# v projected with tokens on partitions, and the second projection's seven products in another order

## The chip, the cores and the metric

The kernel runs on one core of a Trainium2 chip. The metric is the device time of one execution in microseconds (us). Times are medians of several executions on the chip; the profile is one execution more, recorded by the hardware profiler, with a time of its own.

## The reference

One layer of a decoder trunk, all in float32, with 1024 tokens (S) of width 1024 (D). Two branches share one input projection:

```python
mod = silu(c) @ ada_w + ada_b;  shift, scale, gate = split(mod, 3)
h = rms_norm(x, norm_w) * (1 + scale) + shift
gm_u, gm_v, gm_z, ssm_z, xbc, dt_raw, g_a, g_b = split(h @ w_in)
# gMLP branch: layer norm of v over its 1024 columns, then a causal mix over chunks of 128 tokens, per group of 128 columns
v   = layer_norm(gelu(gm_v), gm_ln_w, gm_ln_b)
y_a = gelu(gm_u) * (einsum('gts,bnsgd->bntgd', tril(gm_ws), v) + gm_bs) * silu(gm_z)
# SSD branch: conv, silu, chunked state passing (8 groups, 32 heads), gate, rms norm per group of 256 columns
xbc = silu(causal_depthwise_conv(xbc, conv_w, conv_b))
y_b = (ssd_scan(x, softplus(dt_raw + dt_bias), ...) + x * d_skip) * silu(ssm_z)
y_b = rms_norm(y_b per group, ssm_norm_w)          # width 2048
merged = sigmoid(g_a) * (y_a @ w_proj_a) + sigmoid(g_b) * (y_b @ w_proj_b)
out = rms_norm(x + gate * (merged @ w_out), final_norm_w)
```

The layer norm of v needs, for each token, the mean and variance over all 1024 columns of gelu(v); the mix contracts over the tokens of a chunk, so it wants v with tokens on the 128 partitions.

## The kernel before, in words

**Products.** Large matrix products are split in two ways. Each float32 operand is a sum of a rounded part h and a rest l, and a product is h·h + l·h + h·l, three matmuls on 128x512 tiles. Above that stands a Strassen scheme with seven products instead of eight of half the size (p1 to p7), with sums of the quarters as operands: on the activations' side b11, b22, b21 and t1 to t4, on the weights' side a11, a12, a22 and s1 to s4. One product over 512 rows of the contraction is 12 matmuls (3 times 4 blocks k of 128).

**Stages.** In order of time TensorE does: the norm, the modulation and the first gate products; the input projection; the state passing (SSD) with the first projection (y_a @ w_proj_a) between its steps; the second projection (y_b @ w_proj_b); the output projection, followed by the last norm and the stores.

**Input projection.** A job is a pair of 128-column blocks of w_in (`pair`), made by seven `product` calls, each 12 matmuls at line 574. The weights are the stationary operand, the activations (transposed, tokens along the free dimension) the moving one, so the result has columns on partitions: c1 and c2, 128x1024 each. `pair_weights` loads four 256 KB tiles for a pair (rows of 128 columns, 512 B pieces) and forms the operands on ScalarE (rounded part) and VectorE (rest, line 523, and the sums). The four v pairs come first (v0, v2, v4, v6), then those for B and C, u and z, x, z and the gates.

**v.** `v_done` (L849) applies gelu and hands the block to `v_natural` (L857) twice, some products later (`later(n, f)` calls f after n products; `run_tasks` counts). `v_natural` turns four 128x128 blocks on TensorE into a PSUM bank (tile pv, L84), takes statistics of each on VectorE (L863), copies the bank on ScalarE (L864) and, for the second half, stores v_d[g], 512 KB. `v_stats` (L868) aggregates over the 8 groups; `mix_load` and `mix` read v_d, normalise and mix.

**SSD and its row sums.** For each group `post2` sums squares on TensorE (16 tiny matmuls into a bank called pq), scales on VectorE (L1117) and takes the power -1/2 on POOL (L1121); `post3` turns the 128x8 result into a row on TensorE (pr, L84) and stores it as rs_d[g]. The last two groups (6 and 7) do this within p1 of the second projection.

**Second projection.** 56 units (nm, k), L1418: seven products in the order p1, p5, p2, p3, p6, p7, p4, eight blocks k each. A unit is 12 matmuls (L1477): four PSUM banks, three matmuls a bank. `loads` runs 6 units ahead, `operands` 4. A product uses four banks x or four banks y; p1, p6, p7 and p4 take x, p5, p2 and p3 take y. Fresh quarters of y_b are loaded (yb_d), normalised with the row factors (L1416) and kept in slots; sums of quarters (S and T forms) are made on VectorE. After the last k of a product the banks are copied out (ScalarE) or added to a kept tile (VectorE, L1630 for p2, L1643 for p7). `merged` applies the gates and forms the operands of the output projection. `tha` (L1308) is the end of the first projection's gating: VectorE reads PSUM banks called pma there.

**What sets the order.** TensorE's matmuls and turns stay in the written order. On VectorE, ScalarE and POOL a scheduler orders the instructions by a timeline of its own, except those pinned (`pin`) or given high priority; each engine then executes its list in order. Loads are issued by SP (L90) in its list's order, stores mostly by ScalarE (L93). A load waits until the slot of its pool that it is to fill has been released.

## Time and profile before

| | |
|---|---|
| runs, us | 1407.88, 1404.68, 1408.73 (median 1407.88) |
| profiled execution, us | 1407.67 |
| its span, us | 1405.9 |
| granted clock of TensorE | 0.997 |
| DMA over the span | 283.37 MB, mean 202 GB/s |

The span runs from the first to the last instruction of the profile; the execution's own time is 1.8 us longer. Rows of the timeline give start and duration in us, the engine (PE is TensorE, PEld its weight loads, DVE VectorE, ACT ScalarE, SP the engine that issues loads), the line, the operation, output and inputs by name, the tile, and how many instructions are joined; in brackets the idle time just before and what ended it. A run of matmuls overlaps, so the distance of two starts is the cost of one, not its duration.

### The profile page before, as it was taken

What the parts mean: (1) busy time and instruction counts of PE and PEld (TensorE: products, weight loads), DVE (VectorE), ACT (ScalarE), POOL (GpSimd) and SP (SyncE); (2) the same over time, 40 slices, a digit from 0 to 9 for tenths busy, and PEclk for the clock granted to TensorE, in tenths of its full rate; (3) what the DMA queues carried; (4) which work ended last, traced back from release to release, by engine and by line L of the source; (5) the groups of instructions that cost most, each with busy time, mean ns of one, the idle gap of its engine ahead of it and who ended that gap; (6) DMA issues with size and microseconds to landing.
All of it is one profiled execution on the core that took longest, in us unless ns stands there. A gap on an engine that the chain in (4) does not pass through costs nothing.

```text
span 1405.9 us, 20633 instructions
## 1 busy us (share of the span) xinstructions
PE 1377.1 (98%) x7035; PEld 1139.9 (81%) x7035; DVE 1062.4 (76%) x1863; ACT 797.0 (57%) x1471; POOL 213.0 (15%) x208
## 2 busy tenths in 40 slices
PE   8999999999999999999999999999999999999997
PEld 6688888888888888888887888888888877878886
DVE  4786776777778889889788796388667767876976
ACT  5764576556656665556565555677766723322443
POOL 0000000000000011111000010038778740000001
PEclk9999999999999999999999999999999999999999
DMA  8653343343344777787675774598778749878903
GB/s 263 173 165 98 113 120 105 105 121 120 116 125 134 214 202 239 236 248 232 192 221 156 240 214 135 173 353 318 262 253 296 275 168 328 320 231 296 350 33 120
DMA packets 273150, 283.37 MB, mean 202 GB/s; under 512 B 15341, under 2 KB 223637, under 8 KB 273045
## 3 DMA queue, kind: packets, MB, share of 16 engines
q1 hardware_dynamic: 185684, 198.52, 44.4%
q10 hardware_dynamic: 87360, 83.54, 17.8%
q8 instruction: 55, 0.90, 0.3%
q14 instruction: 51, 0.41, 0.1%
HBM read 194.55 MB, written 87.46 MB: 201 GB/s over the span
## 4 chain that ended last, share of the span: by engine, by line
PE 80%; DMA 8%; DVE 5%; POOL 2%; issue 2%; ACT 1%; SPq 1%; ACTq 0%; DVEq 0%; POOLq 0%
PE xcb L574 6%; PE xuz L574 6%; PE xz L574 6%; PE xx L574 5%; PE xg L574 5%; PE x L1477 4%; PE yp L1477 4%; PE ox L1676 3%; PE yuz L574 3%; PE ycb L574 3%; PE pma L81 3%; PE xv L574 3%; PE yz L574 3%; PE yg L574 3%; PE yx L574 3%; DMA dcy<-acs_d 3%
## 5 line engine op out<-in xcount | busy, mean ns | idle before, releaser
L793 POOL TENSOR_TENSOR wog<-wog,gb 128x256 f32<-128x256 f32 x16 | 18.3, 1159 | 676.6 <-PE zz L574 413.3
L1007 ACT ACTIVATE dcy<-dcy,nacs 128x128 f32<-128x128 f32 x256 | 78.6, 388 | 14.9 <-POOL dcy L1002 14.5
L1002 POOL TENSOR_SCALAR_AFFINE_SELECT dcy<-dcy 128x1024 f32<-128x1024 f32 x32 | 35.0, 1095 | 135.7 <-ACT ea L999 132.3
L999 ACT ACTIVATE ea<-dcy 64x512 f32<-64x512 f32 x64 | 40.1, 626 | 14.2 <-DMA dcy<-acs_d 13.8
L920 ACT ACTIVATE ac<-ac 128x1024 f32<-128x1024 f32 x32 | 33.9, 1060 | 23.0 <-DVE ac L918 22.8
L81 PE MATMUL pma<-yh,wah 128*128 128x512 f32 x128 | 43.3, 419 | 0.0
L1027 DVE TENSOR_TENSOR dcy<-dcy,pc 128x1024 f32<-128x1024 f32 x32 | 39.0, 1218 | 4.8 <-PE pc L84 3.0
L81 PE MATMUL pma<-yh,wal 128*128 128x512 f32 x128 | 42.5, 413 | 0.0
L1089 POOL TENSOR_TENSOR yz<-y,sl 128x512 f32<-128x512 f32 x32 | 41.4, 1295 | 1.1
L1087 DVE TENSOR_TENSOR ym<-yn,ea 128x512 f32<-128x512 f32 (+1 forms) x32 | 19.9, 622 | 28.5 <-PE yn L81 28.3
L81 PE MATMUL pma<-yl,wah 128*128 128x512 f32 x128 | 40.1, 394 | 0.0
L1088 POOL TENSOR_TENSOR y<-y,ym 128x512 f32<-128x512 f32 (+1 forms) x32 | 36.6, 1144 | 14.4 <-DVE ym L1087 14.4
L81 PEld LDWEIGHTS yn<-sl,st 128*128 128x128 f32 x224 | 30.3, 190 | 8.3 <-issue 4.4
L81 PE MATMUL yn<-sl,st 128*128 128x128 f32 x224 | 31.6, 276 | 4.9 <-DVE st L1057 4.9
L1416 DVE SCALAR_TENSOR_TENSOR yn<-yn,par,rb 128x512 f32<-128x512 f32 x32 | 24.0, 749 | 15.7 <-DMA yn<-yb_d 15.5
L81 PE MATMUL sp<-xe,bn 128*128 128x256 f32 x112 | 32.6, 408 | 3.3 <-DVE ssq L1117 1.7
L81 PE MATMUL yi<-dcy,xd 128*64 128x128 f32 x512 | 35.7, 283 | 0.0
L918 DVE SCALAR_TENSOR_TENSOR ac<-c2x,cwt,ac 128x1023 f32<-128x1023 f32 (+2 forms) x24 | 31.2, 1300 | 5.3 <-ACT ac L916 5.1
L918 DVE SCALAR_TENSOR_TENSOR ac<-c2cb,cwt,ac 128x1023 f32<-128x1023 f32 (+2 forms) x24 | 31.1, 1296 | 4.4 <-ACT ac L916 4.3
L1691 POOL TENSOR_TENSOR r<-r,fnw 128x512 f32<-128x512 f32 x2 | 2.5, 1296 | 203.7 <-DMA out_dram<-r 203.7
L1055 POOL TENSOR_TENSOR st<-st,cd 128x256 f32<-128x256 f32 x48 | 32.1, 668 | 8.0 <-PE yn L81 5.3
L918 DVE SCALAR_TENSOR_TENSOR ac<-c1cb,cwt,ac 128x1023 f32<-128x1023 f32 (+2 forms) x24 | 31.6, 1318 | 1.3 <-ACT ac L916 1.3
(2980 smaller groups left out, 4390.9 us busy)
## 6 DMA issues: line engine op xcount, KB each, us to landing
sl<-s_d SPq DMA_DIRECT2D x32, 768.0 KB
s_d<-ac ACTq DMA_DIRECT2D x32, 512.0 KB
dcy<-acs_d SPq DMA_DIRECT2D x32, 512.0 KB
aw<-in_ada_w_dram SPq DMA_DIRECT2D x16, 512.0 KB
wbr<-in_w_proj_b_dram SPq DMA_DIRECT2D x64, 128.0 KB
wb_d<-wbb ACTq DMA_DIRECT2D x32, 256.0 KB
wb_d<-wbc ACTq DMA_DIRECT2D x32, 256.0 KB
yb_d<-yz ACTq DMA_DIRECT2D x32, 256.0 KB
```

What stands on the lines that cost most here:

```text
L81: pin(PE.matmul(acc, l, r, start=first, stop=last))
L574: pin(PE.matmul(ps, lw[:, k * P : (k + 1) * P], r[k], start=first and n + k == 0, stop=n == 2 and k == 3, skip_group_check=not first))
L918: V.scalar_tensor_tensor(ac[:, s:], cc[:, : S - s], conv_wt[:, 3 - s, i : i + 1], ac[:, s:], op0=ALU.mult, op1=ALU.add)
L920: A.activation(ac, ac, AF.Silu)
L999: A.activation(ea[hh * HD : (hh + 1) * HD], dcy.rearrange("p (j e) i l -> p e j (i l)", e=2)[hh * HD : (hh + 1) * HD, hh], AF.Exp)
L1002: G.affine_select(out=d8, in_=d8, compare_op=ALU.is_ge, fill=-1e30, base=0, pattern=[[0, 2 * HPG], [1, P]], channel_multiplier=-1)
L1007: A.activation(dcy[:, h, i, :], dcy[:, h, i, :], AF.Exp, bias=sub[:, i, h : h + 1])
L1027: V.tensor_tensor(d3, d3, pc[:, 0:256].unsqueeze(1).to_broadcast([P, HPG, 256]), op=ALU.mult)
L1088: G.tensor_add(y1[:, :, t0:], y1[:, :, t0:], m[:, :, t0:])
L1089: G.tensor_mul(yz, y1, sl[:, 4:6])
L1477: pin(PE.matmul(ps[j], a[:, v, js], r, start=first and n + k == 0, stop=n == 2 and k == KT - 1, skip_group_check=not first))
L1676: pin(PE.matmul(ps, a[:, tsl], b[:, cs], start=first and n + j == 0, stop=n == 2 and j == 3, skip_group_check=not first))
```

## The change

1. **v.** The four v pairs are replaced by `v_block`. Blocks of the activations are now the stationary operand and rows of w_in (128x512 tiles, 256 KB, 2 KB pieces) the moving one, so the result has tokens on partitions. The same seven products run over 28 units (product, k) in the order p1, p5, p6, p3, p7, p2, p4, each unit 12 matmuls on four banks. Sums of the weights' quarters are made in place in the 8 slots (four of them are kept from p5 to p3); quarters are loaded again where they are needed again, 36 loads of 256 KB instead of 16. The turns of `v_natural`, its copies and its stores go; gelu works on the finished wide tiles, 16 statistics of 512 columns replace 64 of 128, and 16 stores of 256 KB (512 B pieces) fill v_d. `pair_weights` and the loop over the pairs lose their special case for the first pairs.
2. **Row sums.** The scaling in `post2` gets high priority. Groups 6 and 7 do `post2` after units 1 and 2 of p1 (before: 1 and 4) and `post3` after units 3 and 4 (before: 4 and 6).
3. **Second projection.** The order becomes p1, p3, p6, p5, p7, p2, p4, on the banks x, y, x, y, x, y, x. The sums of quarters are formed in place (b12-b11, b22-b12, then b22-b11 and b21-b22), the sums of results too: p1, p3 and p5 are copied out, p6, p5, p7 and p2 added to kept tiles. Banks are taken as three of y, four of x, and the last of y, so pma's banks fall to other positions. `merged` goes through a21, a22, a11, a12, with s1, s2, s3 formed accordingly.

The core of the diff (new and changed lines of `v_block`, `post2`, and the second projection):

```diff
-    def v_done(g):
-        def done(cv):
-            A.activation(cv, cv, AF.Gelu_apprx_tanh)
-            vn = wide(f"vn{g}")
-            later(3 if g < 6 else 2, v_natural, g, cv, vn, 0)
-            later(4 if g < 6 else 3, v_natural, g, cv, vn, 1)
-        return done
-    def v_natural(g, cv, vn, q):
-        pt = bank(f"pv{g}_{q}")
-        for i in range(4):
-            ch = 4 * q + i
-            tp(pt[:, i * P : (i + 1) * P], cv[:, ch * P : (ch + 1) * P], ident)
-        for i in range(4):
-            V.bn_stats(bst[:, 4 * q + i, g, :], pt[:, i * P : (i + 1) * P])
-        A.copy(vn[:, q * 512 : (q + 1) * 512], pt)
-        if q:
-            store(v_d[g], vn)
+    def v_block():
+        V_OPS = (("p1", "b11", "x"), ("p5", "t1", "y"), ("p6", "t2", "x"), ("p3", "b22", "y"), ("p7", "t3", "x"),
+                 ("p2", "b21", "y"), ("p4", "t4", "x"))
+        units = [(nm, k) for nm, _, _ in V_OPS for k in range(4)]
...
+            if nm == "p5":
+                keep(V.tensor_add(t, q[0], t))
+                kept[k] = t
+            elif nm == "p6":
+                t = kept[k]
+                keep(V.tensor_sub(t, t, q[0]))
+            elif nm == "p3":
+                t = kept.pop(k)
+                keep(V.tensor_sub(t, q[0], t))
+            elif nm == "p7":
+                keep(V.tensor_sub(t, q[0], t))
+            hi, lo = wt(f"{nm}v{k}h", "wh", 8), wt(f"{nm}v{k}l", "wl", 8)
+            keep(A.copy(hi, t))
+            keep(V.tensor_sub(lo, t, f32(hi)))
...
+        def ahead():
+            while loaded[0] < len(units) and live[0] + (2 if units[loaded[0]][0] in ("p5", "p7") else 1) <= 8:
+                loads(loaded[0])
+                loaded[0] += 1
+        LEAD = 3
...
+        def finished(nm, i):
+            rows, c = (0, 4)[nm[2] == "2"] + 2 * i, (0, 1)[nm[1] == "2"]
+            w = res[nm][i]
+            A.activation(w, w, AF.Gelu_apprx_tanh)
+            for j in range(2):
+                V.bn_stats(bst[:, rows + j, c, :], w[:, j * 512 : (j + 1) * 512])
+                store(v_d[4 * c : 4 * c + 4].rearrange("g p q -> p g q")[:, :, (rows + j) * P : (rows + j + 1) * P],
+                      w[:, j * 512 : (j + 1) * 512].rearrange("p (g q) -> p g q", g=4))
...
+        for u, (nm, k) in enumerate(units):
+            for j in range(4):
+                js = slice(j * P, (j + 1) * P)
+                (bh, bl), (wh, wl) = (bop[bn][v][k] for v in range(2)), wops[u]
+                for n, (l, r) in enumerate(((bh, wh), (bl, wh), (bh, wl))):
+                    pin(PE.matmul(ps[pn][j], l[:, js], r, start=nm in ("p1", "p5", "p2") and n + k == 0,
+                                  stop=n == 2 and k == 3, skip_group_check=nm not in ("p1", "p5", "p2")))
...
-            V.tensor_scalar(ssq[:, g * NCH + q * 4 : g * NCH + q * 4 + 4], pq[:, 0:4], 1.0 / 256, EPS,
-                            op0=ALU.mult, op1=ALU.add)
+            with tc.high_priority():
+                V.tensor_scalar(ssq[:, g * NCH + q * 4 : g * NCH + q * 4 + 4], pq[:, 0:4], 1.0 / 256, EPS,
+                                op0=ALU.mult, op1=ALU.add)
...
-    units = [(nm, k) for nm in ("p1", "p5", "p2", "p3", "p6", "p7", "p4") for k in range(KT)]
+    units = [(nm, k) for nm in ("p1", "p3", "p6", "p5", "p7", "p2", "p4") for k in range(KT)]
-    fresh = {"p1": (0, 0), "p5": (0, 1), "p2": (KT, 0), "p3": (KT, 1)}
+    fresh = {"p1": (0, 0), "p3": (KT, 1), "p6": (0, 1), "p2": (KT, 0)}
...
-        if nm == "p5":
+        if nm == "p6":
             V.tensor_sub(b12, b12, b11)
-        elif nm == "p6":
-            V.tensor_sub(b12, b22, b12)
-            give(f"yn{KT + k}_1")
+            V.tensor_sub(b22, b22, b12)
         elif nm == "p7":
-            V.tensor_sub(b11, b12, b11)
+            V.tensor_sub(b11, b22, b11)
...
+        elif nm == "p2":
+            give(f"p2r{k}")
+            V.tensor_sub(b21, b21, b22)
+            give(f"yn{KT + k}_1")
...
-    GATES = {"p2": (0, 0), "p6": (0, 1), "p7": (4, 1), "p4": (4, 0)}
+    GATES = {"p5": (0, 1), "p7": (4, 1), "p2": (0, 0), "p4": (4, 0)}
...
-                psy = banks("yp5", "y")
+                psy = banks("yp3", "y", 3)
                 psx = banks("x", "x")
-                rows_bank[0] = lambda name: psy[("pr6", "pr7", "pq6_1", "pq7_1").index(name)]
-            elif nm in ("p2", "p3"):
+                psy += [psb.tile([P, 512], F32, name="yp33", tag="by3")]
+                rows_bank[0] = lambda name: psy[("pq6_1", "pq7_1", "pr6", "pr7").index(name)]
+            elif nm in ("p5", "p2"):
                 psy = banks(f"y{nm}", "y")
...
-        if nm == "p1" and k in (1, 4):
-            late = groups[NG - 2 + k // 4]
+        if nm == "p1" and k in (1, 2):
+            late = groups[NG - 3 + k]
             late.post2(1, late.late)
...
-        if nm == "p1" and k in (4, 6):
-            groups[NG - 4 + k // 2].post3()
+        if nm == "p1" and k in (3, 4):
+            groups[NG - 5 + k].post3()
```

232 lines of the change are left out of this document (130 added, 102 removed).

## The prediction

> **What bounds the kernel now.** I read the page first, for which engine sets the end. In its fence stand the busy time of each engine and the shares of the chain that ended last.
>
> ```profile
> PE 1377.1 (98%) x7035; PEld 1139.9 (81%) x7035; DVE 1062.4 (76%) x1863; ACT 797.0 (57%) x1471; POOL 213.0 (15%) x208
> ...
> PE 80%; DMA 8%; DVE 5%; POOL 2%; issue 2%; ACT 1%; SPq 1%; ACTq 0%; DVEq 0%; POOLq 0%
> ```
>
> TensorE is busy for 1377.1 of the 1405.9 us of the span and carries 80% of the chain. An edit therefore moves the end by the TensorE time that it adds or takes away, or by a wait of TensorE that it makes or removes; work on other engines counts only where TensorE waits for it. The profiled run took 1407.67 us, 0.21 under the median of 1407.88 of the runs shown (1404.68 to 1408.73), so the sum below is made against 1407.67. A change under 0.3% (4.2 us) can't be told from none.
>
> The next view is the timeline of TensorE in the v pairs. A row is start, duration, engine, line, and how many instructions it joins.
>
> ```profile
> 90.05 1.07 PE L574 MATMUL yv<-t1h,p5v2h 128*128 128x512 f32 x4
> ...
> 92.77 0.60 PE L84 MATMUL pv<-ident,c1v 128*128 128x128 f32 x4
> 93.12 1.17 PE L574 MATMUL xv<-t4h,p4v0h 128*128 128x512 f32 x4
> ...
> 95.96 0.60 PE L84 MATMUL pv<-ident,c1v 128*128 128x128 f32 x4
> ```
>
> One product of a pair is twelve matmuls of 128x512 in three rows of four. The product that begins at 90.05 ends where the pv row begins: 2.72 us, 0.227 each. The one that begins with the pv row at 92.77 ends at 95.96, where the next pv begins: 3.19. A group of four turns costs TensorE 0.47 us. All that this stage does besides is seen in the rows of the tile pv (minimum, median and maximum ns, first and last start).
>
> ```profile
> L863 DVE BATCH_NORM_STATS2 bst<-pv x64: 278/282/293, 95.3 to 166.5; 128x6 f32<-128x128 f32 x64
> L84 PE MATMUL pv<-ident,c1v x32: 270/272/275, 92.8 to 161.8; 128*128 128x128 f32 x32
> ...
> L84 PE MATMUL pv<-ident,c2v x32: 270/272/273, 104.6 to 165.4; 128*128 128x128 f32 x32
> L864 ACT COPY vn<-pv x16: 578/587/589, 96.2 to 166.8; 128x512 f32<-128x512 f32 x16
> ```
>
> Last come the windows, for what the other engines and the transfers have left (busy time of PE, PEld, DVE, ACT and POOL, the granted clock, the DMA share, GB/s).
>
> ```profile
> 100.00:170.00 70.00, 70.00 (x337) 57.47 (x337) 46.45 (x124) 35.17 (x56) 0.00 (x0) 1.00 0.34 110
> ...
> 1178.50:1200.00 21.50, 19.81 (x89) 16.07 (x88) 18.93 (x32) 9.01 (x17) 1.65 (x1) 1.00 1.04 393
> ...
> 1222.00:1245.00 23.00, 21.07 (x90) 16.20 (x89) 22.32 (x38) 7.05 (x12) 0.00 (x0) 1.00 0.76 274
> ```
>
> In the v stage VectorE is busy 46 of 70 us and the transfers use a third of their time. In the second projection VectorE is full in one window (22.32 of 23 us), and 393 GB/s has been moved in another. The clock is 1.00 in all.
>
> **The change, part by part.**
>
> *v with tokens on partitions.* The 28 units of the new block hold 12 matmuls each, the same 336 of 128x512 as the four pairs. Whether an operand is the stationary or the moving one doesn't alter their count or shape, and I take 0.227 us each; a unit is 2.72. The 64 turns in 16 groups go: 16 x 0.47 = 7.5 us off TensorE. With them go 16 copies on ScalarE and 48 of 64 statistics on VectorE (the 16 left are four times as wide); both engines were ahead, so these count nothing. Added are 20 loads of 256 KB on SP, so that 9.4 MB are read instead of 4.2, and the eight stores of 512 KB become 16 of half the size on ScalarE's queue. The extra 5.2 MB over 76 us are 68 GB/s on the 110 of the window, 178 in sum, less than half of the 393 seen; the price there is zero unless the slots run dry, which is the first rival.
>
> *The start of the block.* In the kernel before, the first product needs the rounded-off rest of its weights (p1v0l) only at its ninth matmul.
>
> ```profile
> 70.54 1.07 PE L574 MATMUL xv<-b11h,p1v0h 128*128 128x512 f32 x4
> ...
> 76.45 1.07 PE L574 MATMUL xv<-t2h,p6v0h 128*128 128x512 f32 x4
> ```
>
> From 70.54 to 76.45 are two products, 5.91 us where 5.44 would do, so 0.47 was lost already. The new first unit takes its three matmuls bank by bank, so the rest is needed by the third matmul, at 70.54 + 2 x 0.227 = 71.0.
>
> ```profile
> 71.58 0.69 DVE L523 TENSOR_TENSOR p1v0l<-a11v,p1v0h 128x512 fp32r<-128x512 f32 x1
> 72.18 0.68 DVE L529 TENSOR_TENSOR s1v<-a21v,a22v 128x512 f32<-128x512 f32 x1
> ```
>
> VectorE comes to it at 71.58, in the same place of its order in both kernels, and is done at 72.27. With the time to start, TensorE resumes near 72.3: 1.3 us lost instead of 0.47, +0.85. The second unit's rest takes the next place, 72.18, and is done near 72.9; it is needed after 74.5. The operands that follow have over a unit in hand.
>
> *The first product of the second projection.*
>
> ```profile
> 1156.92 0.39 PE L1477 MATMUL x<-p1bh,p1a 128*128 128x512 f32 x1
> ...
> 1158.74 0.39 PE L1477 MATMUL x<-p1bh,p1a 128*128 128x512 f32 x1
> 1160.54 0.50 PE L1477 MATMUL x<-p1bh,p1a 128*128 128x512 f32 x1 [1.41 <-DVE tha L1308]
> ```
>
> ```profile
> 1159.81 1.28 DVE L1308 SCALAR_TENSOR_TENSOR tha<-tha,pma 128x512 f32<-128x512 f32 x2
> ```
>
> The tenth matmul opens the fourth bank and waits 1.41 us, since that bank still holds pma of group 7, which VectorE reads from 1159.81 on. In the new order of banks pma's bank is that of the third instead, three matmuls earlier. The wait ends when it did and begins 3 x 0.227 sooner: +0.68.
>
> *The row sums of groups 6 and 7.* The chain is a VectorE scaling, POOL's power, a turn on TensorE.
>
> ```profile
> 1175.78 0.27 PE L84 MATMUL yp<-ident,ssq 128*8 128x128 f32 x1
> ...
> 1183.21 0.27 PE L84 MATMUL yp<-ident,ssq 128*8 128x128 f32 x1 [1.69 <-POOL ssq L1121]
> ```
>
> ```profile
> 1174.59 0.68 DVE L1456 TENSOR_TENSOR p1bl<-yn,p1bh 128x512 fp32r<-128x512 f32 x1
> ...
> 1181.27 0.15 DVE L1117 TENSOR_SCALAR ssq<-yp 128x4 f32<-128x4 f32 x1
> ```
>
> ```profile
> 1181.51 1.65 POOL L1121 TENSOR_TENSOR ssq<-ssq,nhalf 128x8 f32<-128x8 f32 x1 [12.90 <-DVE ssq L1117]
> ```
>
> TensorE waits 1.69 us at 1183.21 since the scaling stood late in VectorE's order: done 1181.42, then POOL 1.65 us to 1183.16. The change asks for both sums earlier (after units 1 and 2 instead of 1 and 4) and the turns after units 3 and 4. The scaling then stands behind the eighth p1bl, which began at 1174.59 and gives way about 0.6 later (as 71.58 to 72.18 above), so 1175.2 + 0.15; with the same 0.1 and 1.65 the power is ready near 1177.1. TensorE reaches the second turn after five units and both sums, the point at which it stands at 1175.78 in the row above, plus 0.68 from the bank, some 1176.5. A wait of 0.65 is left: -1.05. Ends: -1.69 (no wait) and 0.
>
> *The borders between products.*
>
> ```profile
> 1229.38 0.39 PE L1477 MATMUL yp<-p2bh,p2a 128*128 128x512 f32 x1
> 1230.41 0.47 PE L1477 MATMUL yp<-p3bh,p3a 128*128 128x512 f32 x1 [0.64 <-issue]
> ...
> 1231.56 0.50 PE L1477 MATMUL yp<-p3bh,p3a 128*128 128x512 f32 x1 [0.22 <-DVE c L1630]
> ...
> 1233.36 0.50 PE L1477 MATMUL yp<-p3bh,p3a 128*128 128x512 f32 x1 [0.84 <-DVE c L1630]
> ...
> 1234.56 0.49 PE L1477 MATMUL yp<-p3bh,p3a 128*128 128x512 f32 x1 [0.23 <-DVE c L1630]
> ```
>
> After p2's last matmul at 1229.38 the next could begin at 1229.61; the tenth matmul of p3 begins at 1234.56, where 9 x 0.227 = 2.04 would put it at 1231.65. So 2.9 us are lost: p3 takes the banks of the product just ahead, and VectorE, full in that window, is late in adding p2 up from them. The new order alternates x,y,x,y,x,y,x; each set of banks has a whole product, 21.8 us, to be emptied, and no such wait is left: -2.9.
>
> ```profile
> 1298.06 0.39 PE L1477 MATMUL x<-p4bh,p4a 128*128 128x512 f32 x1
> ...
> 1300.57 0.51 PE L1477 MATMUL x<-p4bh,p4a 128*128 128x512 f32 x1 [0.24 <-DVE p L1643]
> ```
>
> Likewise p4 behind p7: the tenth matmul starts at 1300.57 and could have at 1298.06 + 2.04 = 1300.10, so -0.5. In the new order p2 stands between them.
>
> The sums in place move VectorE's and ScalarE's work about, not its amount by more than a few instructions. In p7, p2 and p4 I count about 110 VectorE instructions of 128x512 in the changed file. The full window above did 38 in 22.32, 0.59 each, so 110 take 64.6 us beside 24 x 2.72 = 65.3 of TensorE: full, but operands lead by four units (10.9 us), so I take nothing, with an upper end in the second rival. Between the stages both kernels have the same order on every engine; the state passing and the output projection I leave as they are.
>
> **Sum:** -7.5 + 0.85 + 0.68 - 1.05 - 2.9 - 0.5 = -10.4, which gives 1407.67 - 10.4 = **1397.3 us**, 0.7% faster. With the free ends (no wait at the start and none at the turn) it is -11.9, 1395.8; with no gain at the turn 1398.3.
>
> **Rivals.**
>
> *The v block runs dry (slower).* Its 28 units share eight slots. In p5 to p3 four of them are held by sums kept in place, and p7 loads two quarters a unit; a load starts only when VectorE has freed a slot, and SP issues in order, so one late release holds back all behind it.
>
> ```profile
> 62.23 0.50 SPq L90 DMA_DIRECT2D a22v<-in_w_in_dram  x1
> 62.78 0.50 SPq L90 DMA_DIRECT2D a12v<-in_w_in_dram  x1
> ...
> 1167.27 0.32 SPq L90 DMA_DIRECT2D yn<-yb_d  x1
> ```
>
> ```profile
> 1169.90 0.75 DVE L1416 SCALAR_TENSOR_TENSOR yn<-yn,par,rb 128x512 f32<-128x512 f32 x1 [3.01 <-DMA yn<-yb_d]
> ```
>
> A 256 KB load issued at 1167.27 let VectorE go on at 1169.90: 2.6 us. A unit that sees a whole landing loses 2.6. The gain is eaten up at 4 such units, and from 6 on the kernel is slower by more than 0.3%; if the eight units of p3 and p7 wait, 8 x 2.6 = 20.8, and 1397.3 + 20.8 = 1418. Against it: SP issues such loads 0.55 us apart (62.23, 62.78), so landings overlap; and each load is asked for when the operand four units earlier has been formed, 10.9 us ahead, four landings long. Chance 0.13. [...]
>
> *VectorE sets the pace in p7, p2, p4 (no change).* At 0.69 us each, the whole duration of the VectorE row at 71.58, the 110 take 75.9, 10.6 over TensorE's 65.3. If the lead is used up when p7 begins, all is given back: 1407.9. For it: the full window in p3. Against: that window kept 0.59, and the products p3, p6, p5 ahead ask less. Chance 0.07.
>
> *The borders don't gain (smaller gain).* The second projection's waits come back elsewhere: both turns wait as long as before, and p6, whose units load 256 KB of y, as much of row factors every other time and 512 KB of weights just behind p3's like loads, starts as late as p3 did. Then only the v part counts, with the bank: -7.5 + 0.85 + 0.68 = -6.0, 1401.7. For it: at 0.92 MB in 2.72 us that is 337 GB/s, above the first and third of the windows shown; against: 393 GB/s were moved without starving TensorE of operands. Chance 0.10.
>
> **How the numbers follow.** My forecast has 0.70: the terms are waits that the trace shows, each with its cause removed, and the largest is work taken off the engine that is full. Faster is that and the third rival, 0.80; same is the second, 0.07; slower is the first, 0.13. The range: at the low end 1395.8 less 3.0 for the lower of the runs shown (1404.68 against 1407.67), 1392.8; at the high end it takes in the third rival with 1.1 of run spread (1408.73 against 1407.67) and the part of the second in which half the lead is lost, 1397.3 + 5.3 = 1402.6, so 1403. That leaves out the first rival and half of the second, under 2 in 10.
>
> **What would show it.** No pv tile, one wait of TensorE near 1.3 for p1v0l and none after it until the block ends, near 70.5 + 28 x 2.72 + 1.3 = 148. In the second projection a wait of about 2.1 at p1's seventh matmul, one under 0.9 at the second turn, none at the borders; the output projection as long as before. A wait of TensorE on v's quarters with a DMA behind it would make the forecast wrong by the first rival; VectorE waits at p2's or p4's units by the second; more time per matmul with swapped operands (over 0.227) by none of them, at 3.4 us for each hundredth.

## The result, and the profile after

The changed kernel takes 1402.55 us (median of 9 runs) against 1407.0 for the kernel before beside it: ratio 0.9967, 95% interval 0.9952 to 0.9983. A second set gave 1402.41, 0.9966 (0.9954 to 0.9978). It is faster, by 4.5 to 5.7 us in the medians where 10.4 were predicted, and not for the reason that the sum gave the most weight to. The profiled execution took 1405.65 us with a span of 1403.9; that of the repeat (e1) took 1401.54, which is nearer to the median.

The v block did in its place what the prediction said. Its start and its end in TensorE's timeline of the changed kernel:

```profile
70.47 0.40 PE L914 MATMUL vx<-p1v0h,b11h 128*128 128x512 f32 x1
...
72.25 0.50 PE L914 MATMUL vx<-p1v0l,b11h 128*128 128x512 f32 x1 [1.15 <-DVE p1v0l L850]
...
147.85 0.39 PE L914 MATMUL vx<-p4v3l,t4h 128*128 128x512 f32 x1
148.08 1.07 PE L536 MATMUL xcb<-b11h,p1cb0h 128*128 128x512 f32 x4
```

One wait, for p1v0l, and none up to the end at 148.08, against the 148 written down.

The second projection runs from its first matmul to the first of the output projection (`ox`); the last row is the only wait of TensorE that the list of waits has between the two.

```profile
1160.21 0.39 PE L1548 MATMUL x<-p1bh,p1a 128*128 128x512 f32 x1
...
1162.92 0.50 PE L1548 MATMUL x<-p1bh,p1a 128*128 128x512 f32 x1 [1.19 <-DVE tha L1378]
...
1176.26 0.27 PE L84 MATMUL yp<-ident,ssq 128*8 128x128 f32 x1
...
1179.20 0.27 PE L84 MATMUL yp<-ident,ssq 128*8 128x128 f32 x1
...
1318.08 0.39 PE L1741 MATMUL ox<-ma11h 128*128 128x512 f32 x1
```

```profile
PE x L1548 <- DVE tha L1378: 1.2, 1, 1.2
```

It lasts 157.87 us instead of 163.51 (1156.92 to 1320.43): -5.64. No wait is left at a border, and none at the turns.

What the prediction did not look at lies between the two. Four pairs by the start of their first product, before and then after:

```profile
194.51 0.84 PE L574 MATMUL xx<-b11h,p1x0h 128*128 128x512 f32 x3
...
513.52 1.07 PE L574 MATMUL xx<-b11h,p1x4h 128*128 128x512 f32 x4
...
684.88 1.07 PE L574 MATMUL xz<-b11h,p1z3h 128*128 128x512 f32 x4
...
898.73 1.07 PE L574 MATMUL xg<-b11h,p1g14h 128*128 128x512 f32 x4
```

```profile
188.49 0.84 PE L536 MATMUL xx<-b11h,p1x0h 128*128 128x512 f32 x3
...
511.31 1.07 PE L536 MATMUL xx<-b11h,p1x4h 128*128 128x512 f32 x4
...
687.18 1.07 PE L536 MATMUL xz<-b11h,p1z3h 128*128 128x512 f32 x4
...
900.36 0.84 PE L536 MATMUL xg<-b11h,p1g14h 128*128 128x512 f32 x3
```

The changed kernel is 6.02 us ahead at x0, 2.21 at x4, and 2.30 behind at z3. From x4 to z3 lie nine pairs; before they take 171.36 us, 19.04 each, with no wait at all; after 175.87. The waits of TensorE between 460 and 720 us, of which the kernel before has none in this profile, say where:

```profile
PE xuz L536 <- DVE c2uz L552: 1.9, 1, 1.9
PE xz L536 <- DVE c2z L552: 1.4, 2, 1.1
PE xcb L536 <- DVE c2cb L552: 1.0, 1, 1.0
PE xx L536 <- DVE c2x L552: 0.5, 1, 0.5
```

All are of one kind. A pair's product p4 is held back until p1 and p5 of the next pair are done, and adds to the bank from which VectorE has first to take p7 (the addition c2<-p5,x). That addition comes too late. The largest, in VectorE's timeline and then in TensorE's:

```profile
465.00 1.29 DVE L726 SCALAR_TENSOR_TENSOR gacc<-ag,sc,gacc 128x1024 f32<-128x1024 f32 x1 [3.60 <-DMA ag<-in_ada_w_dram]
466.21 1.28 DVE L984 SCALAR_TENSOR_TENSOR ac<-c2x,cwt,ac 128x1022 f32<-128x1022 f32 x1
...
474.40 0.68 DVE L552 TENSOR_TENSOR c2uz<-p5uz,xuz 128x512 f32<-128x512 f32 x1
```

```profile
475.13 1.81 PE L536 MATMUL xuz<-t4h,p4uz7h 128*128 128x512 f32 x4 [1.89 <-DVE c2uz L552]
476.74 1.91 PE L536 MATMUL xuz<-t4l,p4uz7h 128*128 128x512 f32 x4
478.45 1.30 PE L536 MATMUL xuz<-t4h,p4uz7l 128*128 128x512 f32 x4
479.59 0.62 PE L536 MATMUL xcb<-t2h,p6cb4h 128*128 128x512 f32 x2
```

VectorE stands 3.60 us for a load of the gate's weights (ag), has work without a gap from 465.00 on, and reaches the addition at 474.40. In the kernel before the list is the same and the wait is 0.65:

```profile
468.10 1.28 DVE L764 SCALAR_TENSOR_TENSOR gacc<-ag,sc,gacc 128x1024 f32<-128x1024 f32 x1 [0.65 <-DMA ag<-in_ada_w_dram]
```

TensorE's wait of 1.89 us lies ahead of x4 and belongs to this execution: in e1 VectorE stands 1.48 us for the same load, TensorE does not wait, and x0 to x4 takes 319.06 us, against 319.01 before and 322.82 in the profile of after. The waits that the list has behind x4 come to 2.9 us of the 4.51 lost there. A wait in the list is idle time only; at cb5, for one of 0.99, p4 starts 1.15 us late and the row behind it another 0.13.

So the profile of after is accounted for: -6.02 to x0, +7.65 from there to g14, +1.66 in the state passing, -5.64 in the second projection, +0.35 behind it: -2.0, the 1405.65 against 1407.67. The repeat e1: -5.99, +4.17, -1.09, -3.06, -0.1.

### The profile page after: what moved, and what is told of

Same layout as the page of the kernel before. It is cut to its first block, busy times and chain, and to the rows that moved or that the text cites. A ratio compares the mean times of both kernels' runs of the same rounds, so it can differ in the third digit from the quotient of the medians.

```text
span 1403.9 us, 20510 instructions
## 1 busy us (share of the span) xinstructions
PE 1371.6 (98%) x6971; PEld 1134.5 (81%) x6971; DVE 1053.8 (75%) x1815; ACT 787.1 (56%) x1459; POOL 212.4 (15%) x208
## 4 chain that ended last, share of the span: by engine, by line
PE 67%; DMA 13%; DVE 9%; ACT 4%; issue 4%; POOL 2%; SPq 2%; ACTq 0%; DVEq 0%; POOLq 0%
PE xuz L536 6%; PE x L1548 6%; PE xcb L536 5%; PE yp L1548 5%; PE xx L536 4%; PE xz L536 4%; DMA wbr<-in_w_proj_b_dram 3%; PE vx L914 3%; PE xg L536 3%; PE yuz L536 3%; PE ycb L536 3%; PE pma L81 2%; PE ox L1741 2%; DMA dcy<-acs_d 2%; PE yx L536 2%
## 5 line engine op out<-in xcount | busy, mean ns | idle before, releaser
L948 ACT ACTIVATE vm<-vm,vr 128x128 f32<-128x128 f32 x64 | 25.8, 484 | 14.0 <-DMA vm<-v_d 13.5
```

## The experiments

"The middle" is the stretch from x4 to z3, whose undisturbed length is 171.36 us; "loss" is what is over that. "Margin" is the time from the end of VectorE's addition of p7 to the start of p4. For the pair z2, before and then after, VectorE's row and TensorE's:

```profile
630.32 0.67 DVE L590 TENSOR_TENSOR c2z<-p5z,xz 128x512 f32<-128x512 f32 x1
```

```profile
633.20 1.07 PE L574 MATMUL xz<-t4h,p4z2h 128*128 128x512 f32 x4
```

```profile
633.52 0.67 DVE L552 TENSOR_TENSOR c2z<-p5z,xz 128x512 f32<-128x512 f32 x1
```

```profile
634.25 1.19 PE L536 MATMUL xz<-t4h,p4z2h 128*128 128x512 f32 x4 [1.11 <-DVE c2z L552]
```

Before, p4 starts 2.21 us after the addition has ended; after, it waits 1.11 and starts 0.06 behind it. All the profiles:

| kernel | time as a ratio to before (95% interval) | loss in the middle | margin from z1 to g6 |
|---|---|---|---|
| before (profile; e4) | 1 | 0.0; 1.3 | 2.0 to 3.9; 0.2 to 2.0 |
| after; e1 | 0.9967; 0.9966 | 4.5; 5.3 | 0.05 to 0.4; 0.05 to 0.3 |
| e2 v alone | 1.0014 (0.9998, 1.0029) | 6.4 | 0.05 to 0.3 |
| e3 second projection alone | 0.9964 (0.9951, 0.9977) | 1.2 | 1.5 to 3.8 |
| e5 after, padded | 1.0003 (0.9990, 1.0017) | 3.2 | 0.05 to 0.4 |
| e6 before, fewer turns | 1.0023 (1.0005, 1.0040) | 3.5 | 0.05 to 1.7 |
| e16 before, padded | 1.0069 (1.0047, 1.0091) | 0.7 | 0.05 to 2.4 |
| e17 after, same count | 1.0030 (1.0012, 1.0049) | 4.9 | 0.04 to 0.4 |
| e9 after, one tap | 0.9932 (0.9916, 0.9947) | 0.0 | 3.0 to 4.6 |
| e10 e3, one tap | 0.9951 (0.9938, 0.9964) | 0.0 | 2.9 to 4.1 |
| e7; e8 GpSimd sums | 0.9963; 0.9977 | 4.6; 6.3 | 0.04 to 0.8; 0.05 to 0.2 |
| e11; e12 fewer transfers | 0.9951; 0.9989 | 3.5; 2.2 | 0.05 to 1.0; 0.05 to 0.8 |
| e13; e14 p4 later | 1.0056; 1.0068 | other waits | 5.2 to 6.1; 5.1 to 6.1 |
| e15 all three | 1.0061 | other waits | 3.2 to 5.2 |
| e18 one piece | 0.9970 (0.9953, 0.9987) | 6.1 | 0.05 to 2.4 |

**The change again, its parts, and the kernel before again.** e2 has v_block alone, e3 the order of the second projection and the priority of the row sums' scaling alone.

```diff
 e2:    units as before   ("p1", "p5", "p2", "p3", "p6", "p7", "p4")     v_block()
 e3:    units as changed  ("p1", "p3", "p6", "p5", "p7", "p2", "p4")     jobs v0, v2, v4, v6 as before
```

> The changed kernel once more, nothing altered, for a second profile. In the first profile its v part (from 70.5 us to the start of pair x0) came out 6.0 us shorter and its second projection 5.6 us shorter than before, but pairs z0 to g8 (about 467 to 690 us) lost 8.3 us and the state passing 1.7 us, on instruction orders that are the same in both kernels. Theory N (landings vary from run to run, the loss is a draw): the v part and the second projection repeat within 0.5 us, the loss in the middle comes out elsewhere and by another amount, and the times spread over more than 5 us. Theory S (the loss belongs to the kernel): the waits for c2uz, c2cb, c2z and c2x return at the same pairs, loss between 6 and 10 us again. Time by either about 1402.5, within 1398 to 1407.

> Only v with tokens on partitions; second projection, its order, banks and the row sums as before. If the parts add and the middle is undisturbed: -6.0, ratio 0.9957. Theory S, the loss in the middle (7.6 us in the profile) comes with the v block: -6.0 + 6 to 8, ratio 1.000 to 1.0015, and the waits at 475 and 594 us show in the profile. Theory N: some loss in some runs, ratio about 0.998.

> Only the second projection's order with its banks and row sums; v by pairs and turns as before. The profile should show p1 to the output projection 5.6 us shorter (157.9 instead of 163.5). Theory S (loss from the v block): -5.6, ratio 0.996, and the pairs from z0 to g8 as in the kernel before. Theory N: ratio 0.996 to 0.998, with waits in the middle in some runs.

> The kernel before once more, nothing altered, for a second profile: how far one program's middle (pairs z0 to z7, then the state passing) moves from one profiled execution to the next. Theory N: starts of the pairs differ by several us between its two profiles, beginning with a landing. Theory S: they agree within 1 us.

Measured: e1 1402.41, e2 1409.22, e3 1401.84, against 1408.08; e4, a single run, 1405.68. The second projection alone gives all of the gain, -6.2 us in the medians. The v part, worth nothing in the total, is nevertheless 5.7 us short in its own place (e2 starts the block 1.35 late and is 4.39 ahead at x0). It is given back in the middle: 6.4 us. In e1 the waits for c2z, c2cb and c2x came back and that for c2uz did not; its loss of 5.3 us in the middle is below the 6 to 10 expected from z0 to g8, and its second projection is 3.06 us shorter, not 5.64. The kernel before is not free of the same wait either: e4's middle takes 172.67 us, 1.31 over the 171.36, with one wait in the list, at the p4 of z0:

```profile
PE xz L574 <- DVE c2z L590: 1.0, 1, 1.0
```

**The hour or the layout?** Nothing between x0 and the SSD stage stands in another order in the two kernels. By the traces VectorE, GpSimd, SP and TensorE have the same order from x0 to g14. Two things differ there: TensorE arrives 6 us earlier (A, "by the hour"), and buffer slots, DMA lanes and the places of instruction fetches are shifted (B, "by the layout"): v's loads number 36 instead of 16, the first load of cb behind x0 signals its landing on semaphore 107 before and 102 after, and the fetches are measured below. e5 pads the changed kernel, e6 takes three of four turns out of the kernel before (its statistics and copies read the block that is not turned), e16 pads the kernel before. The fences of the edits from here on show their core, `...` marks lines left out.

```diff
 e5, v_block:   -            for j in range(4):
                +            twice = k == 0 and nm in ("p5", "p2")
                +            for j4 in range(8 if twice else 4):
                ...
 e6, v_natural: -            for i in range(4):  tp(pt[:, i * P ...], cv[...], ident)
                +            tp(pt[:, 0:P], cv[:, 4 * q * P : (4 * q + 1) * P], ident)
                ...
 e16, pair:     ...
                +        product(px, ops["p1"], "b11", times=2 if name in ("v2", "v4") else 1)
```

> The changed kernel with 24 extra matmuls in the v block: the first 12 of p5 and the first 12 of p2 are made twice, the second time from zero, so the result is the same. 24 x 0.227 = 5.4 us of TensorE work ahead of x0; the order of every engine from x0 on is as in the changed kernel. Two theories of where the v part's 6 us went. (A) By the hour: something that does not follow TensorE sets when the work of the middle (about 460 to 690 us) can be done, and a TensorE that arrives 6 us early waits for it. Then with 5.4 us of padding x0 starts about 0.5 us before that of the kernel before, the loss between x4 and z3 (4.5 and 5.3 us in the two profiles of the changed kernel) falls to under 1.5 us, and the total stays within about 1.5 us of the changed kernel's 1402.4. (B) By the layout: the v part shifts buffer slots, DMA lanes and the places where instructions are fetched, and VectorE is held longer for landings in the middle whatever the hour. Then the loss of 4.5 to 5.3 us stays, and the total is 1402.4 + 5.4 = about 1407.8.

> The kernel before with 48 of the 64 turns of v left out (three of four of each group; the values that go to v_d and to the statistics are then not turned): TensorE has 48 x 0.118 = 5.6 us less to do ahead of the projections, and the number of instructions and transfers of the other engines, the order of SP and the second projection stay as before. (A) By the hour: x0 starts 5.6 us early, the middle loses 4 to 5 us again as in the changed kernel, and the total is 1406 to 1407.5, within 1.5 us of the kernel before. (B) By the layout: the loss does not appear (under 1.5 us between x4 and z3, as in the profiles of the kernel before), and the total is 1407.5 - 5.6 = about 1402.

> The kernel before with the first products of two v pairs made twice (24 x 0.227 = 5.4 us more TensorE work ahead of the projections; the result is the same). The stage from x0 on is then the same in order, buffers, DMA lanes and fetches, only 5.4 us later. If only the engines' places to one another count, VectorE's margin at p4 stays 1 us and more, the middle loses under 1.5 us, and the total is before + 5.4 = about 1412. If the hour counts (A), the middle changes: it loses 3 us or more (1415 and above), or a delayed TensorE finds everything landed and gets time back (under 1410).

Measured: e5 1407.82 (before 1406.76), loss 3.2 at the old hour; e6 1410.14, loss 3.5 in the old layout, its total above both expectations (1406 to 1407.5 and 1402); e16 1417.08 (before 1406.78), loss 0.7 at an hour 5.54 later. TensorE's rows of e5 and of e16 at x4 and z3:

```profile
513.53 0.84 PE L536 MATMUL xx<-b11h,p1x4h 128*128 128x512 f32 x3
...
688.13 1.07 PE L536 MATMUL xz<-b11h,p1z3h 128*128 128x512 f32 x4
```

```profile
519.06 1.07 PE L574 MATMUL xx<-b11h,p1x4h 128*128 128x512 f32 x4
...
691.07 1.07 PE L574 MATMUL xz<-b11h,p1z3h 128*128 128x512 f32 x4
```

(A) falls: e5 is at x4 within 0.01 us of the kernel before and loses 3.2 all the same, and e16 comes 5.5 us later and loses almost nothing. (B) as worded falls with e6, which loses without the v block. e16's total is 5 us over the 1412 expected: 3.2 of them appear in its profile in the state passing, whose length differs from that of the kernel before by -3.4 (e8) to +3.2 us and of which no theory spoke.

One companion was left: the large instruction fetches (queue q8 of the page, 55 of 16 KB in either profile; by their number, one to some 255 of the matmuls and weight loads, they are put down to TensorE), at 444 to 450 us in the kernels that lose little (449.5 before) and at 458 to 464 in most others (463.6 after), by the transfer records (on a clock set so that x0 starts where it does in the kernel before).

```diff
 e17, v_block:  +                for i in range(64):
                +                    pin(PE.matmul(ps["y"][0][:, 0:2], bop["t1"][0][...], wops[u][0][:, 0:2], start=True, stop=True))
```

> The changed kernel with 64 matmuls of two columns ahead of p5 of the v block (their result is written over): TensorE then has as many instructions ahead of the projections as in the kernel before, which has 64 turns there. In the traces the large instruction fetches (16 KB, one about every 29.5 us) fall, counted from TensorE's x0, at 444 to 450 us in the four profiles of kernels that lose under 1.3 us in the middle with all the work done (before, before again, the second projection alone, before padded) and at 458 to 464 us in the five that lose 3 us or more (changed, changed again, v alone, changed padded, fewer turns). If that place is the cause and not only a companion, the fetch goes back to 444 to 451 us, the margin at p4 is over 0.2 us and the loss between x4 and z3 under 1.5 us (4.5 and 5.3 in the changed kernel). If it is only a companion, the loss stays at 3 to 6 us. The total says little: 1402.4 plus the 64 matmuls (2 to 7.5 us), less 4 us or not.

Measured: the fetch falls at 449.7 (457.9 less the 8.19 by which x0 is late), the loss is 4.9, the total 1412.18 (before 1409.6). A companion only; and not even that in e8 (449.6, loss 6.3) and e9 (462.2, loss 0.0), which follow.

**Does VectorE's margin decide?**

```diff
 e9, e10, conv_done:  -            for s in (1, 2, 3):
                      +            for s in (1,):
```

> The changed kernel with two of the three shifted taps of each convolution left out (the values are then not those of the reference): 64 additions of 1.30 us on VectorE are gone, about 5.2 us from each convolution pair (x, cb); TensorE, the transfers and the side work stay. Two theories of what makes the stage from 460 to 690 us lose time after the v block. (C) VectorE's margin: VectorE, held for landings, has no time to spare there, so its addition of p7 comes too late for p4. Given 2.6 us a pair, it has: the margin is over 1 us everywhere from 574 to 672 us, the loss between x4 and z3 (4.5, 5.3) falls to under 1 us, and the total goes to 1394 to 1397.5. (D) The transfers: SP's loads, queued behind one another and behind landings, bring the weights late whatever VectorE's load; then the loss stays at 3 us or more and the total is above 1399.

> The same two taps left out of the kernel that has the second projection's new order and not the new v (1401.84 whole). There VectorE's margin is already 1.5 to 3.8 us, so under (C) only its few single waits go: 1399.5 to 1401.5, and the v part, taken as e9 against this run, is worth 4 to 6 us, about what it gains in its own place (5.4 to 6.0). Under (D) both kernels move alike and the v part is still worth 0 +- 1.5.

Measured: e9 1394.90, e10 1399.28. Of e9, TensorE at x0, x4 and z3, and z2's addition with its p4:

```profile
187.90 0.84 PE L536 MATMUL xx<-b11h,p1x0h 128*128 128x512 f32 x3
...
506.91 1.07 PE L536 MATMUL xx<-b11h,p1x4h 128*128 128x512 f32 x4
...
626.59 1.07 PE L536 MATMUL xz<-t4h,p4z2h 128*128 128x512 f32 x4
...
678.27 1.07 PE L536 MATMUL xz<-b11h,p1z3h 128*128 128x512 f32 x4
```

```profile
622.88 0.68 DVE L552 TENSOR_TENSOR c2z<-p5z,xz 128x512 f32<-128x512 f32 x1
```

e9 is 6.61 us ahead at x0, 6.61 at x4 and 6.61 at z3; no wait at p4 is left in either kernel. The v part, e9 against e10, is now worth 4.4 us in the medians (3.2 in the means of six runs each, and the intervals of the two ratios overlap), and 6.6 in the two profiles up to z3. This is what (C) expected and not what (D) did: where VectorE's addition is done 3 us ahead of p4, the middle loses nothing, and up to z3 the v part pays about the 6.65 that were predicted of it. One thing else changes with the taps: the scheduler lays VectorE's list anew. Of the 789 instructions besides the taps between x0 and g14, 335 stand at another place of the list in e9 than in the changed kernel (the same in e10 against e3); in e5, e6, e16 and e17 none does. Less work and another order were not tried apart. The windows from 500 to 690 us, before, after and then e9, show how little it takes (busy time of PE, PEld, DVE, ACT, POOL, clock, DMA share, GB/s):

```profile
500.00:690.00 190.00, 190.00 (x840) 157.39 (x839) 163.98 (x294) 108.17 (x185) 22.49 (x18) 1.00 0.78 235
```

```profile
500.00:690.00 190.00, 187.14 (x820) 153.22 (x819) 157.22 (x287) 102.35 (x180) 21.53 (x18) 1.00 0.76 230
```

```profile
500.00:690.00 190.00, 190.00 (x844) 157.52 (x843) 147.39 (x285) 110.32 (x188) 21.96 (x18) 1.00 0.78 232
```

VectorE is not full in the changed kernel, 157 of 190 us, and less busy than in the kernel before, 164. In the rest it stands, in the order of its list, mostly for transfers and for ScalarE. From VectorE's waits between 555 and 675 us, before (its longest) and after (its three longest):

```profile
DVE wba L830 <- ACT wba L825: 1.9, 2, 1.1
```

```profile
DVE wog L766 <- DMA wo_d<-wog: 5.7, 2, 4.0
DVE wba L792 <- ACT wba L787: 4.2, 4, 1.8
DVE s1g L525 <- DMA a22g<-in_w_in_dram: 2.5, 2, 1.8
```

**Can the margin be had with all the work done?** e7 and e8 take the wait for the store of wog off VectorE.

```diff
 e7, e8, gated_sums:  -            V.tensor_sub(r4[:, d], r4[:, a], r4[:, b])
                      +            G.tensor_sub(r4[:, d], r4[:, a], r4[:, b])
```

> The changed kernel with the four subtractions of each of the eight units of gated output weights (gated_sums) on GpSimd instead of VectorE; nothing else is changed. VectorE no longer stands behind the store of those weights (waits of 3.4 to 5.7 us in the window 555 to 675 us in the two profiles of the changed kernel) and has 8 x 4 x 0.42 = 13 us less work in the middle. If VectorE, held for landings, is what makes TensorE wait at p4 for the addition of p7 (c2): the margin between that addition and p4, 0.05 to 0.4 us from 572 to 672 us in the changed kernel, grows to over 1 us, the loss between x4 and z3 falls from 4.5 to 5.3 us to under 2, and the total goes to 1397 to 1399.5. If the waits at p4 come from something else (the loads of the weights, ScalarE's copies), the loss stays and the total stays at 1402. [...]

> The same edit (gated_sums on GpSimd) on the kernel that has the second projection's new order and not the new v. There VectorE's margin at p4 is 1.5 to 3.8 us between 577 and 672 us and TensorE loses little in the middle, so if the edit works by giving VectorE back its margin it is worth at most 1 us here: 1401 to 1402 (1401.84 without it). Then the v part, taken between this run and the one before it, is worth 3 to 5 us instead of nothing. If the edit helps both alike, the v part is still worth nothing and the cause lies elsewhere.

Measured: 1402.33 and 1403.47 (before 1406.76), both expectations of a gain missed. VectorE's waits for a22 of the z pairs rose to 5.8 us between 500 and 690 us in e7, and the kernel that had a margin lost it (6.3 us in e8): one wait taken away, the next took its place. By the words of its expectation e7, with the loss at 4.6 and the total unchanged, speaks for another cause than VectorE's work; what it shows is that 13 us less of it do not bring the margin back. Here too the list is laid anew, as in all the runs that follow (in e7, 101 of the 757 instructions common to both kernels stand elsewhere).

e11 and e12 join the wbb and wbc pieces of a quarter and two of the loads of a gated unit; e18 makes a quarter one piece.

```diff
 e11, e12:  -        wb_parts(i, "wbb", 0, 2, raw[:, 2:4])
            -        wb_parts(i, "wbc", 2, 2, raw[:, 0:2])
            +        wb_parts(i, "wbb", 0, 4, raw)
            ...
            +        load(r4[:, 2:4], w_out[(j + 4) * P : (j + 5) * P].rearrange("p (c q w) -> p q c w", c=2, q=2)[:, q])
 e18:       ...
            +        V.tensor_add(s, a22, a21)          # s: fifth part of raw
            +        A.copy(hl[:, :, 0], raw)           # all five parts, then one subtraction and one store
```

> The changed kernel with the side work of the middle in fewer pieces and the same bytes: the two copies, two subtractions and two stores of each wb quarter (wbb, wbc) become one of each, twice as wide, and two of the four loads of each gated unit become one; 40 transfers, 64 instructions of ScalarE and 32 of VectorE fewer in all, and VectorE's and ScalarE's busy time hardly changes. In the waits of SP between 500 and 690 us, its loads stand 17 to 27 us for the landing of the wbc stores and 9 to 13 for those of wbb, transfers that they have no data from. If the number of transfers in flight is what delays the loads (D), SP's waits fall, the loss between x4 and z3 falls from 4.5 to 5.3 us to under 2.5, and the total goes to 1398 to 1400. If only VectorE's own load counts (C), the loss stays within 1 us of what it was and the total at 1401.5 to 1402.5.

> The same edit on the kernel with the second projection's new order alone (1401.84). It loses little in the middle, so 1400.5 to 1402 under either theory. The v part, e11 against this run: 2 to 5 us faster under (D), 0 +- 1 under (C).

> The changed kernel with the fewer transfers of e11 taken one step further and the first unit's order of e15: a wb quarter is one copy, one subtraction and one store of all five parts (the first sum goes to a fifth place, so that a22 stays for p4), instead of two of each in e11 and three in the changed kernel. Against the changed kernel VectorE has 64 instructions fewer in the middle at about 0.14 us of fixed cost each (0.28 us for 128 columns, 0.42 for 256 in its rows), some 9 us, ScalarE 128, the transfers 72; and VectorE no longer stands for ScalarE's copy of wba (4.2 to 7.0 us between 500 and 690 us). If VectorE's margin is the cause (C), the loss between x4 and z3 falls below 2 us, and with 1.1 us from the first unit the total is 1394.5 to 1397.5. If the margin is eaten by other landings, it is 1397.5 to 1399 as in e11.

Measured: e11 1398.99 (0.9951, 0.9939 to 0.9963), e12 1404.35 (0.9989, 0.9978 to 1.0000), before 1406.19; e18 1404.36 (before 1409.6). e11 is the quickest kernel here with all the work done, though its interval overlaps that of the changed kernel. The v part is worth 5.4 us between e11 and e12, but only since e12 came out slower than e3 (0.9989 against 0.9964). The expected mechanism is not borne out: e11 still loses 3.5 us in the middle, e12 2.2 instead of 1.2. e18 has less work and fewer transfers than either and still loses 6.1; VectorE's two longest waits between 500 and 690 us are these:

```profile
DVE wog L767 <- DMA wo_d<-wog: 10.3, 4, 3.5
DVE wbr L794 <- DMA wbr<-in_w_proj_b_dram: 7.9, 6, 2.4
```

e13 and e14 move the point at which TensorE needs the addition; e15 adds e11's edit and another order of the first unit.

```diff
 e13, e14, e15, pair:  -        if pending:
                       -            pending.pop()()
                                product(px, ops["p6"], "t2", False)
                                out(A.copy, c1[:, 512:1024], px)
                                after(2)
                       +        if pending:
                       +            pending.pop()()
 e15, v_block:         ...
                       +            for j, n in sorted(((j, n) for j in range(4) for n in range(3)), key=lambda t: u == 0 and t[1] == 2):
```

> The changed kernel with the held-back product p4 of a pair made one product later, after p6 of the next pair instead of after its p5: VectorE's addition of p7 may come 2.72 us later before TensorE waits for it. All the work stays. If the waits at p4 are what eats the v part's gain (C), the margin before p4 grows by 2.7 us to over 1 us nearly everywhere, the loss between x4 and z3 falls from 4.5 to 5.3 us to under 2, and the total goes from 1402.4 to 1397 to 1399.5. If VectorE is short of time by 0.6 us a pair for good and not only late now and then, the 2.7 us are used up after five pairs and the total falls to 1400 to 1401 only.

> The same edit on the kernel with the second projection's new order alone (1401.84), where p4 waits little (under 1.3 us between x4 and z3, some 2 us in all): 1400 to 1401.8. The v part, e13 against this run, is then worth 2 to 4.5 us; if the edit helps both alike it is worth 0 +- 1 and the p4 wait is not the cause.

> The changed kernel with p4 one product later, the fewer transfers of the run before (1398.99 alone), and the first unit of the v block ordered so that its four products with the low part of the weights come last of the twelve (that part lands late: a wait of 1.15 us there in the profile of the changed kernel). If all three add up, 1.1 us at the start and most of what is left of the loss in the middle go: 1394.5 to 1397. If e13 and the fewer transfers gave the same microseconds, 1397 to 1398.5.

Measured: 1415.47, 1416.33, 1414.74 (before 1406.78); a miss, and mine. The margin rose to over 5 us in e13 and e14 as meant, and e13's waits of TensorE between 300 and 700 us are these:

```profile
PE xx L536 <- ACT c1x L552: 5.1, 4, 3.2
PE xcb L536 <- ACT c1cb L552: 3.0, 3, 1.2
PE xz L536 <- ACT c1z L552: 1.2, 1, 1.2
```

The held-back p4 had also been the cover of ScalarE's copy of p1, which must be done before p6 adds to the same bank: with p4 moved, one product lies between p1 and p6 instead of two. So the three say nothing on what the wait at p4 costs.

**What stays open.** Where the time goes is shown: TensorE stands at p4 for VectorE's addition, in every kernel that loses 3 us or more with p4 in its place. That the wait goes when the addition comes early is shown by e9 and e10 alone, by less work and another order of it together. With all the work done, nothing tried here took the loss away (e7, e11 and e18 keep it, e13 puts other waits in its place). Why the kernel before has the margin is not shown. It is not the hour (e5, e16) and not the place of the instruction fetches (e17); fewer transfers and less VectorE work do not suffice (e18). It does not take the v block to lose it: e6 and e8 lose 3.5 and 6.3 us without. The kernel before stands close to the edge itself: from z1 to g6 its margin is between 0.2 and 3.9 us in two profiles, and at z0 the second has 0.06 and a wait. The slots and lanes, which the v block's 36 loads shift, weren't varied by themselves.

## Why the prediction was right and wrong

- **The v block** was right. Predicted -6.65 at its end (-7.5 and +0.85); at x0 the profiles show -6.0 (after, e1), -5.7 (e2, from its own start), -6.6 (e9, e13). The wait at the start was 1.15 where 1.3 was written. Part of the rest is a wait of TensorE for ScalarE's copy c1uz of 0.3 us. The rival of slots that run dry did not come about: after 72.25 TensorE waits for nothing in the block.
- **The borders** were right: p2, p3 and p4 of the second projection took 22.56, 24.02 and 22.37 us before and 21.76 each after, -3.7 where -3.4 was predicted.
- **The bank and the turns** were mis-sized, to the good. Predicted +0.68 and -1.05, measured together -1.9: the wait for tha came earlier by three matmuls but was 1.19 instead of the 2.1 expected, since VectorE was done with pma earlier, and the second turn did not wait at all. It is not steady: 2.25 and no turn in e1, no wait for tha and a turn of 1.2 in e3. VectorE did not set the pace in p7, p2 and p4: 103 instructions, 62.24 of 65.28 us, where about 110 and 64.6 were counted.
- **The step that failed** is the sentence "Between the stages both kernels have the same order on every engine", and the zero that it stood for. The order is the same; the time is not. Of the 7.65 us lost between x0 and g14 in the profile (4.17 in e1) the sum had none. In its place the runs show TensorE waiting at p4 for VectorE's addition of p7: 3.2 to 6.4 us are lost between x4 and z3 in the five profiles with the v block and otherwise all the work as it was (after, e1, e2, e5, e17), against 0.0 and 1.3 in the two of the kernel before. The prediction read windows in the v stage and in the second projection only. The window from 500 to 690 us of the kernel before shows TensorE at 190.00 of 190 us, VectorE at 163.98 and the transfers at 0.78, and the margin of 2.2 us at the p4 of z2 stood in the timeline. Why the v block uses that margin up is open.
- **The likeliest case** was therefore wrong by 5 us, and the time inside the range. It came out near the third rival's 1401.7, by the opposite path, which is luck: there the v part was to be kept and the second projection lost; here the second projection was kept and the v part lost.

## What to carry to other kernels

Time taken off the busiest engine in one stage reaches the end only if every later stage can take it (here 6.02 us ahead at x0 were 2.30 behind at z3): look, in each, for the tightest hand-over to that engine (here VectorE's addition before p4), measure its margin in the timeline, and count a stage with a margin like the one here (0.2 to 3.9 us from z1 to g6 in the two profiles of the kernel before) as one that may give the gain back. The same order of instructions is no proof of the same time: from x0 to x4 two executions of the changed kernel took 322.82 and 319.06 us, and VectorE, which works its list in order, stood 3.60 and 1.48 us in them for the same load. Two edits can be tried apart cheaply, and where one seems to be worth nothing, a kernel with work left out behind it (e9) tells a useless edit from a useful one that is hidden.

## What was not expected of the hardware

A wait of 1.89 us was followed by a stretch at a granted clock of 0.50. The twelve matmuls from 475.13 to 479.59 take 4.46 us instead of 2.72, and the windows around them show the granted clock:

```profile
465.00:475.00 10.00, 8.25 (x37) 6.50 (x35) 10.00 (x15) 4.81 (x9) 0.00 (x0) 1.00 0.61 199
475.00:485.00 10.00, 9.87 (x36) 7.98 (x37) 8.28 (x19) 6.49 (x11) 0.00 (x0) 0.83 0.55 151
```

In windows of 1 us the clock is 0.74 from 475, 0.50 from 476 and 477, 0.55 from 478 and 1.00 again from 479: 3.4 us at 0.50, some 1.7 us of time on top of the wait. In e1 the wait of 2.25 us for tha was followed by the same 0.83 (1155 to 1165). The waits of 1.11 and 1.19 us in the changed kernel were not: 1.00 in the 10 us from 634.25 and from 1162.92. But the length of the wait alone does not decide: in e7 one of 1.56 us, up to 1127.09, with shorter gaps around it, was followed by a clock of 0.83 (1124 to 1134 us), in e16 one of 3.26 us, up to 1193.12, was not (1.00 from 1186 to 1202). What else decides is not shown.

In e17 the clock fell without a wait: the 64 matmuls of two columns take 11.43 us (83.17 to 94.60), and in the window from 84 to 100 us TensorE is busy for all 16.00 us at a granted clock of 0.57; over the whole profile it is 0.993, in that of the kernel before 0.997.

The last surprise is how far a landing moves with the same order of instructions: the load of ag that VectorE waits for was issued at 459.73 and let it go on at 465.00, 5.3 us, in the changed kernel, and 464.04 to 468.10, 4.1 us, in the kernel before. What moved it was not looked for.
